# Masking the diagonal score blocks and swapping the maxima on other engines, in a hybrid decoder block

## The chip, the cores and the metric

The kernel runs on one core of a Trainium2 chip. The metric is the device time of one execution in microseconds (us). The core has a matrix engine (TensorE, PE in the rows; its weight loads are PEld) and three others: VectorE (DVE), ScalarE (ACT) and GpSimd (POOL). SyncE (SP) issues DMAs. Each engine works its own queue in order and waits for semaphores of the others. TensorE writes to PSUM, which VectorE and ScalarE read; GpSimd works in SBUF alone.

## The reference, cut to what matters

One decoder block on 1040 tokens (16 meta tokens and 1024 of the sequence) of width 1024: RMSNorm, one wide input projection, a pooling branch and an attention branch, gates, an output projection, and a final RMSNorm. The change is in the attention: 8 heads of width 64, with a forget gate that adds a difference of cumulated log gates to every score, and a causal mask:

```python
s = jnp.einsum('bqhd,bkhd->bhqk', qb, kb).astype(jnp.float32) * scale
s = s + c[:, :, q0:q1, None] - c[:, :, None, :q1]
valid = (k_idx <= q_idx) & ((k_idx >= pad) | (k_idx == q_idx))
s = jnp.where(valid, s, -jnp.inf)
p = jax.nn.softmax(s, axis=-1)
outs.append(jnp.einsum('bhqk,bkhd->bqhd', p.astype(vb.dtype), vb))
```

## The kernel before, in words

All products are made in pieces of reduced precision: a float32 operand is split into a high part (a copy on ScalarE) and a low part (a subtraction on VectorE or GpSimd), and three products (high with low, low with high, high with high) are summed in PSUM.

The attention is worked in 16 units: 4 pairs of heads, 2 heads in a pair, 2 halves of 512 queries (`Unit`, L537). Scores are kept transposed: 128 keys on the partitions, queries on the free axis. A unit of the first half has 5 blocks of keys, one of the second half 9. The queries of a half begin 16 tokens after a block of keys, so a block of keys on the diagonal covers 112 or 128 (for the last block 16) queries that need a mask; block `b` is computed from column `c0` on, and `d1` is where its masked columns end. In each unit:

- `qk(b)` (L557): two products into a bank `ps` of two (`psS`). Then the scores are moved to the tile `s` in SBUF with the key's gate sum `negc` added. The columns under the mask go through VectorE, which adds the constant tile `mask` in the same instruction (L579); the others go through ScalarE (L581). Then VectorE takes the running maximum over the blocks, `m` (L585, L586, L588). The last block of the second half (`own_keys`) is the 16 queries' own keys, with a mask of its own, `tail`.
- `maxes` (L590): the maximum over the 128 keys of each query. VectorE transposes `m` in squares of 32 (L593), reduces (L595), and joins the partitions: it copies the two halves of 64 partitions crosswise (L597), takes the maximum (L598), copies the quarters of 32 crosswise (L600), takes the maximum (L601), and broadcasts the result by a transpose into a PSUM bank, `pm` (L603).
- `soft(b)` (L606): VectorE subtracts `pm` (L612), ScalarE takes the exponential (L613) and the high part `ph` (L616), VectorE makes the low part `pl` (L617), and GpSimd adds into the unit's sums `acc` (L622 to L625). Two blocks later `av` (L629) multiplies both parts with the values into the bank `po`.
- `finish` (L636): ScalarE and VectorE join the halves of `po` (L640, L641) and it is stored; VectorE transposes and reduces the sums (L644, L646).

The scores of the next unit run between the softmax blocks of the current one (`merged`, L649). TensorE's order is as written. Between the attention's products it gets filler: projections (`g_proj`, L155) that `F.pull(ns)` (L355) draws from a queue for a given time, for instance `LM1` before and `LM2` behind the maxima. The projections use three banks `pj`, and each chunk of weights is split by ScalarE (L140) and GpSimd (L124, in four pieces). The order of instructions on the other engines, and of the DMAs on their queues, is made by a planner from data dependencies, the order of the text and its own costs of the instructions. The matmuls, their order and the calls of `F.pull` are the same in both kernels.

The mask constants are made at the start (L82 to L91).

Of the kernel before, what the change touches and what calls it, by code (L numbers as in the profile page):

```python
# [8 lines left out]
F32 = mybir.dt.float32  # L9
F32R = mybir.dt.float32r  # L10
AF = mybir.ActivationFunctionType
ALU = mybir.AluOpType
# [9 lines left out]
NEG = -1e30  # L22
KB = 128
# [29 lines left out]
def tile_hybrid_block(ctx, tc, x, meta, norm_g, w_in, b_forget, pool_w, pool_scale,  # L53
                      w_up_pool, w_up_attn, w_out, final_g, out):
    nc = tc.nc
# [8 lines left out]
    cst = ctx.enter_context(tc.tile_pool(name="cst", bufs=1))  # L64
# [14 lines left out]
    make_identity(nc, ident)  # L79
    epsp = cst.tile([128, 1], F32, name="epsp")  # L80
    nc.vector.memset(epsp, -0.5)
    mask = cst.tile([KB, KB], F32, name="mask")  # L82
    nc.vector.memset(mask, 0.0)
    nc.gpsimd.affine_select(out=mask, in_=mask, pattern=[[1, KB]], compare_op=ALU.is_ge, fill=NEG,
                            base=0, channel_multiplier=-1)
    tail = cst.tile([KB, OWN], F32, name="tail")
    nc.vector.memset(tail, 0.0)
    nc.gpsimd.affine_select(out=tail, in_=tail, pattern=[[1, OWN]], compare_op=ALU.is_ge, fill=NEG,
                            base=KB - OWN, channel_multiplier=-1)
    nc.gpsimd.affine_select(out=tail, in_=tail, pattern=[[0, OWN]], compare_op=ALU.is_ge, fill=NEG,  # L90
                            base=OWN - KB, channel_multiplier=1)  # L91
# [3 lines left out]
                            base=OWN - KB, channel_multiplier=1)  # L95
# [441 lines left out]
    class Unit:  # L537
# [19 lines left out]
        def qk(self, b):  # L557
            p, e, q0, t0, kb, c0 = self.p, self.e, self.q0, self.t0, self.kb[b], self.c0[b]
            h = 2 * p + e
            ka, qa, ql = KA[p, e], QA[p, e], QL[p, e]  # L560
            d1 = max(0, min(512, b * KB + KB - t0))
            own_keys = b == NB - 1
            if b == 0:
                self.m = ap_.tile([KB, 512], F32, name="m")
            m = self.m
            if b % 2 == 0:
                self.st = ap_.tile([KB, 2, 512], F32, name="S", tag="s", bufs=6)
            s = self.st[:, b % 2, :]
            self.S.append(s)
            ps = psS.tile([128, 512], F32, name="ps")  # L570
            k0 = KS[b]
            nc.tensor.matmul(ps[:kb, c0:], ka[:, k0:k0 + kb], qa[:, q0 + c0:q0 + 512], start=True, stop=False)  # L572
            nc.tensor.matmul(ps[:kb, c0:], ka[:, k0:k0 + kb], ql[:, q0 + c0:q0 + 512], start=False, stop=True)  # L573
            nb_ = negc[:kb, b, h:h + 1]
            f0 = max(d1, c0)
            if d1 > c0:
                j = t0 + c0 - b * KB
                mk = tail if own_keys else mask[:, j:j + d1 - c0]
                nc.vector.scalar_tensor_tensor(s[:kb, c0:d1], ps[:kb, c0:d1], nb_, mk, op0=ALU.add, op1=ALU.add)  # L579
            if f0 < 512:  # L580
                nc.scalar.activation(s[:kb, f0:], ps[:kb, f0:], AF.Identity, bias=nb_)  # L581
            S0 = self.S[0]
            if b == 1:
                if c0:
                    nc.vector.tensor_copy(m[:, :c0], S0[:, :c0])  # L585
                nc.vector.tensor_tensor(m[:, c0:], S0[:, c0:], s[:, c0:], op=ALU.max)  # L586
            elif b > 1:
                nc.vector.tensor_tensor(m[:kb, c0:], m[:kb, c0:], s[:kb, c0:], op=ALU.max)  # L588

        def maxes(self, extra=0.0):  # L590
            F.pull(LM1 + extra)
            mt = ap_.tile([KB, 512], F32, name="mt")
            nc.vector.transpose(mt, self.m)  # L593
            r, x, r2, y, mx = [sm.tile([128, 16], F32, name=n) for n in ("mr", "mx", "ms", "my", "mz")]
            nc.vector.tensor_reduce(r, mt.rearrange("p (j b) -> p j b", b=32), axis=AX.X, op=ALU.max)  # L595
            for a, b in ((0, 64), (64, 0)):
                nc.vector.tensor_copy(x[a:a + 64], r[b:b + 64])  # L597
            nc.vector.tensor_tensor(r2, r, x, op=ALU.max)  # L598
            for a, b in ((0, 32), (32, 0), (64, 96), (96, 64)):
                nc.vector.tensor_copy(y[a:a + 32], r2[b:b + 32])  # L600
            nc.vector.tensor_tensor(mx, r2, y, op=ALU.max)  # L601
            self.pm = psT.tile([128, 512], F32, name="pt")
            nc.vector.transpose(self.pm, mx[:, :, None].to_broadcast([128, 16, 32]))  # L603
            F.pull(LM2)
# [347 lines left out]
    for n, s in enumerate(steps):  # L952
# [12 lines left out]
        j, a = s  # L965
# [84 lines left out]
    for n in range(7):  # L1050
        if n < 6:
            prep(n + 1)
        ps = ba if n in (0, 2, 4, 6) else bb_
# [56 lines left out]
```

## Time and profile before

| | |
|---|---|
| median of 3 runs | 744.31 us (744.23 to 744.82) |
| the profiled execution's own time | 743.96 us |
| its span, first to last instruction | 742.2 us |
| TensorE busy | 731.2 us (99%) |
| VectorE busy | 533.2 us (72%) |
| ScalarE busy | 377.0 us (51%) |
| GpSimd busy | 332.8 us (45%) |
| granted TensorE clock, mean | 0.997 |

The span is the time between the first and the last instruction that the profiler saw on the core. Busy time is the time in which an engine has an instruction under way; matmuls are pipelined, so a TensorE that is busy need not be at its peak. The attention runs from about 84 to 505 us, with projections between its products. The time before belongs to the norm and the first projections, the time after it to the branches, gates and the output projection.

### The profile page before, as it was taken

How to read it: one execution, taken by the hardware profiler on the slowest of the kernel's cores; microseconds unless marked ns; L12 is line 12 of the kernel's file. 1: busy time of each engine (PE TensorE's matmuls, PEld its weight loads, DVE VectorE, ACT ScalarE, POOL GpSimd, SP SyncE). 2: the span in 40 equal slices, each digit the busy share in tenths (PEclk: the TensorE clock that was granted, in tenths of full speed). 3: DMA queues.
4: the chain of work that ended last, by engine and by line, in shares of the span. 5: the costliest groups of instructions: out<-in, count | busy, mean ns of one | idle time of the engine just before them, and what ended most of it. 6: DMA issues, size and time to landing. Idle time of an engine off the chain costs nothing.

```text
span 742.2 us, 10619 instructions
## 1 busy us (share of the span) xinstructions
PE 731.2 (99%) x3686; PEld 622.7 (84%) x3686; DVE 533.2 (72%) x991; ACT 377.0 (51%) x736; POOL 332.8 (45%) x390
## 2 busy tenths in 40 slices
PE   8999999999999999999999999999999999999996
PEld 5997999988888898889988888888887888888885
DVE  5653577668779877688797687686288554997975
ACT  6662556446557545556563564452545322526445
POOL 4331235456426446345355383183348043606743
PEclk9999999999999999999999999999999999999998
DMA  9301132231312212222323223229375357360006
GB/s 301 88 15 43 29 86 86 62 98 23 95 48 60 80 50 90 78 53 55 94 66 86 80 80 92 72 81 309 95 201 212 142 200 240 116 224 1 1 0 227
DMA packets 76424, 75.35 MB, mean 102 GB/s; under 512 B 9665, under 2 KB 60865, under 8 KB 76370
## 3 DMA queue, kind: packets, MB, share of 16 engines
q1 hardware_dynamic: 74496, 69.95, 30.8%
q10 hardware_dynamic: 1874, 4.72, 1.7%
q8 instruction: 29, 0.48, 0.3%
q14 instruction: 25, 0.20, 0.1%
HBM read 55.58 MB, written 19.07 MB: 101 GB/s over the span
## 4 chain that ended last, share of the span: by engine, by line
PE 87%; DVE 5%; ACT 1%; issue 1%; POOLq 0%; POOL 0%; ACTq 0%
PE pj L152 65%; PE pj L995 8%; PE po L633 5%; PE ps L573 2%; PE ps L572 2%; PE pt L995 2%; PE pj L486 1%; DVE S L612 1%; DVE pl L617 1%; DVE ka L266 0%; PE pj L279 0%; DVE pt L603 0%; ACT S L581 0%; DVE mt L593 0%; ACT whi L140 0%
## 5 line engine op out<-in xcount | busy, mean ns | idle before, releaser
L124 POOL TENSOR_TENSOR wlo<-raw,whi 128x256 fp32r<-128x256 f32 x148 | 121.7, 852 | 192.5 <-ACT whi L140 96.1
L152 PE MATMUL pj<-hh,whi 128*128 128x512 f32 (+4 forms) x768 | 178.4, 360 | 0.6 <-ACT hh L201 0.3
L152 PE MATMUL pj<-hl,whi 128*128 128x512 f32 (+4 forms) x768 | 177.1, 359 | 0.0
L152 PE MATMUL pj<-hh,wlo 128*128 128x512 f32 (+4 forms) x768 | 174.4, 358 | 0.0
L152 PEld LDWEIGHTS pj<-hh,wlo 128*128 128x128 f32 x768 | 132.3, 188 | 18.1
L152 PEld LDWEIGHTS pj<-hh,whi 128*128 128x128 f32 x768 | 131.5, 188 | 18.7 <-ACT hh L201 0.5
L152 PEld LDWEIGHTS pj<-hl,whi 128*128 128x128 f32 x768 | 131.6, 188 | 17.7
L617 DVE TENSOR_TENSOR pl<-S,ph 128x512 fp32r<-128x512 f32 (+4 forms) x112 | 87.1, 792 | 19.3 <-ACT ph L616 18.8
L625 POOL TENSOR_TENSOR acc<-acc,S 128x272 f32<-128x272 f32 (+4 forms) x80 | 76.7, 958 | 11.2 <-ACT S L613 6.0
L581 ACT ACTIVATE S<-ps,negc 128x400 f32<-128x400 f32 (+2 forms) x96 | 49.3, 515 | 44.0 <-DVE S L579 35.7
L613 ACT ACTIVATE S<-S 128x512 f32<-128x512 f32 (+4 forms) x112 | 49.5, 478 | 33.7 <-DVE S L612 33.5
L616 ACT ACTIVATE ph<-S 128x512 fp32r<-128x512 f32 (+4 forms) x112 | 52.2, 480 | 15.8 <-PE po L633 14.4
L588 DVE TENSOR_TENSOR m<-m,S 128x272 f32<-128x272 f32 (+4 forms) x80 | 41.3, 517 | 23.8 <-ACT S L581 22.0
L140 ACT ACTIVATE whi<-raw 128x1024 fp32r<-128x1024 f32 x37 | 39.1, 1056 | 32.2 <-PE pj L152 27.8
L612 DVE TENSOR_TENSOR S<-S,pt 128x512 f32<-128x512 f32 (+4 forms) x112 | 51.9, 498 | 0.8
L836 DVE TENSOR_TENSOR rl<-pj,rl 128x512 f32<-128x512 f32 x32 | 22.0, 689 | 28.0 <-PE pj L152 28.0
L579 DVE SCALAR_TENSOR_TENSOR S<-ps,negc,mask 128x128 f32<-128x128 f32 (+2 forms) x72 | 23.7, 330 | 22.5 <-PE ps L573 22.3
L317 ACT ACTIVATE st<-pj 128x512 f32<-128x512 f32 x40 | 23.7, 593 | 28.1 <-PE pj L152 18.6
L633 PE MATMUL po<-pl,V 128*128 128x512 f32 (+4 forms) x112 | 37.6, 336 | 0.1
L573 PE MATMUL ps<-ql,ka 128*128 128x512 f32 (+4 forms) x112 | 37.5, 334 | 0.0
L572 PE MATMUL ps<-qa,ka 128*128 128x512 f32 (+4 forms) x112 | 36.0, 322 | 0.6 <-ACT S L581 0.5
L995 PE MATMUL pj<-opy 128*128 128x512 f32 (+1 forms) x168 | 36.3, 375 | 0.0
(187 smaller groups left out, 1134.2 us busy)
## 6 DMA issues: line engine op xcount, KB each, us to landing
raw<-in_w_in_dram SPq DMA_DIRECT2D x40, 512.0 KB, 3.9
sp_gp<-st SPq DMA_DIRECT2D x16, 256.0 KB, 2.0
sp_ga<-st SPq DMA_DIRECT2D x16, 256.0 KB, 2.0
rl<-sp_gp SPq DMA_DIRECT2D x8, 512.0 KB, 5.2
rl<-sp_ga SPq DMA_DIRECT2D x8, 512.0 KB, 4.5
W<-in_w_out_dram SPq DMA_DIRECT2D x8, 512.0 KB, 4.8
xr<-in_x_dram SPq DMA_DIRECT2D x8, 512.0 KB, 4.1
xt<-in_x_dram SPq DMA_DIRECT2D x7, 512.0 KB, 8.1
```

What stands on the lines that cost most here:

```text
L124: ins = nc.gpsimd.tensor_tensor(out[:, c:c + 256], x[:, c:c + 256], y[:, c:c + 256], op=op)
L152: nc.tensor.matmul(ps, a, b, start=(i == 0), stop=(i == len(seq) - 1))
L572: nc.tensor.matmul(ps[:kb, c0:], ka[:, k0:k0 + kb], qa[:, q0 + c0:q0 + 512], start=True, stop=False)
L573: nc.tensor.matmul(ps[:kb, c0:], ka[:, k0:k0 + kb], ql[:, q0 + c0:q0 + 512], start=False, stop=True)
L581: nc.scalar.activation(s[:kb, f0:], ps[:kb, f0:], AF.Identity, bias=nb_)
L612: nc.vector.tensor_tensor(s[:kb, c0:], s[:kb, c0:], self.pm[:kb, c0:], op=ALU.subtract)
L613: exps.append(nc.scalar.activation(s[:kb, c0:], s[:kb, c0:], AF.Exp))
L616: nc.scalar.activation(ph[:kb, c0:], s[:kb, c0:], AF.Copy)
L617: dves.append(nc.vector.tensor_tensor(pl[:kb, c0:], s[:kb, c0:], r32(ph[:kb, c0:]), op=ALU.subtract))
L625: nc.gpsimd.tensor_tensor(acc[:kb, c0:], acc[:kb, c0:], s[:kb, c0:], op=ALU.add)
L633: nc.tensor.matmul(self.po[:, c0:], v, r[:kb, c0:], start=(b == 0 and i == 0), stop=(b == self.nb - 1 and i == 1))
L995: nc.tensor.matmul(ps, pick(A_, k, p)[:, i * 128:(i + 1) * 128], pick(B_, k, q)[:, c0:c1], start=start and n == 0, stop=n == 11, skip_grou ...
```

## The change

The masked columns of a block are no longer moved by VectorE with the mask added. ScalarE moves the whole block, from `c0` to the end, and GpSimd then overwrites, in place in SBUF, the columns `c0` to `d1` where the key is later than the query with -1e30 (an affine select: it keeps an element where an affine form of partition and column is not negative). The `own_keys` block stays on VectorE. The constant `mask` goes. In `maxes` the six crosswise copies of a unit become activations of ScalarE. The rest is the same.

```diff
-    mask = cst.tile([KB, KB], F32, name="mask")
-    nc.vector.memset(mask, 0.0)
-    nc.gpsimd.affine_select(out=mask, in_=mask, pattern=[[1, KB]], compare_op=ALU.is_ge, fill=NEG,
-                            base=0, channel_multiplier=-1)
...
             nb_ = negc[:kb, b, h:h + 1]
-            f0 = max(d1, c0)
-            if d1 > c0:
-                j = t0 + c0 - b * KB
-                mk = tail if own_keys else mask[:, j:j + d1 - c0]
-                nc.vector.scalar_tensor_tensor(s[:kb, c0:d1], ps[:kb, c0:d1], nb_, mk, op0=ALU.add, op1=ALU.add)
-            if f0 < 512:
-                nc.scalar.activation(s[:kb, f0:], ps[:kb, f0:], AF.Identity, bias=nb_)
+            if own_keys:
+                nc.vector.scalar_tensor_tensor(s[:, c0:], ps[:, c0:], nb_, tail, op0=ALU.add, op1=ALU.add)
+            else:
+                nc.scalar.activation(s[:, c0:], ps[:, c0:], AF.Identity, bias=nb_)
+                if d1 > c0:
+                    nc.gpsimd.affine_select(out=s[:, c0:d1], in_=s[:, c0:d1], pattern=[[1, d1 - c0]],
+                                            compare_op=ALU.is_ge, fill=NEG, base=t0 + c0 - b * KB,
+                                            channel_multiplier=-1)
...
             for a, b in ((0, 64), (64, 0)):
-                nc.vector.tensor_copy(x[a:a + 64], r[b:b + 64])
+                nc.scalar.activation(x[a:a + 64], r[b:b + 64], AF.Copy)
             nc.vector.tensor_tensor(r2, r, x, op=ALU.max)
             for a, b in ((0, 32), (32, 0), (64, 96), (96, 64)):
-                nc.vector.tensor_copy(y[a:a + 32], r2[b:b + 32])
+                nc.scalar.activation(y[a:a + 32], r2[b:b + 32], AF.Copy)
```

## Rows read from the trace of the kernel before

**Rows 1.** The page, busy us by engine: share of the span, instructions.
```profile
PE 731.2 (99%) x3686; PEld 622.7 (84%) x3686; DVE 533.2 (72%) x991; ACT 377.0 (51%) x736; POOL 332.8 (45%) x390
```
**Rows 2.** Windows: start:end, length, busy us (instructions) by engine, TensorE's clock, DMA.
```profile
84.00:505.00 421.00, 420.09 (x2151) 366.30 (x2151) 328.46 (x686) 230.33 (x478) 202.87 (x229) 1.00 0.26 74
```
**Rows 3.** Waits of TensorE, 84 to 505 us: total us, times, longest.
```profile
PE ps L572 <- ACT S L581: 0.5, 1, 0.5
PE pj L152 <- DVE V L285: 0.2, 1, 0.2
```
**Rows 4.** Tile ps: idle before its instructions, by releaser (us, times).
```profile
  DVE S L579: 35.7, 35
...
  ACT S L581: 1.9, 4
```
**Rows 5.** The page, groups: count, busy us, mean ns, idle before by releaser.
```profile
L579 DVE SCALAR_TENSOR_TENSOR S<-ps,negc,mask 128x128 f32<-128x128 f32 (+2 forms) x72 | 23.7, 330 | 22.5 <-PE ps L573 22.3
```
**Rows 6.** Groups by form, 84 to 490 us, VectorE's crosswise copies.
```profile
L600 DVE COPY my<-ms 32x16 f32<-32x16 f32 x64 | 11.2, 175 | 1.1
...
L597 DVE COPY mx<-mr 64x16 f32<-64x16 f32 x32 | 8.2, 255 | 0.8
```
**Rows 7.** Groups by form, 84 to 490 us, ScalarE.
```profile
L581 ACT ACTIVATE S<-ps,negc 128x512 f32<-128x512 f32 x32 | 21.8, 685 | 8.1 <-PE ps L573 7.8
...
L581 ACT ACTIVATE S<-ps,negc 128x16 f32<-128x16 f32 x16 | 4.3, 269 | 8.2 <-DVE S L579 8.2
...
L613 ACT ACTIVATE S<-S 128x16 f32<-128x16 f32 x16 | 3.3, 208 | 3.2 <-DVE S L612 3.2
```
**Rows 8.** Timeline of GpSimd, 0 to 12 us: start, length, instruction, idle before.
```profile
1.32 0.29 POOL L84 TENSOR_SCALAR_AFFINE_SELECT mask<-mask 128x128 f32<-128x128 f32 x1
1.56 0.20 POOL L88 TENSOR_SCALAR_AFFINE_SELECT tail<-tail 128x16 f32<-128x16 f32 x1
...
5.96 0.55 POOL L114 TENSOR_TENSOR rstd<-rstd,epsp 128x1 f32<-128x1 f32 x1 [4.08 <-DVE rstd L113]
```
**Rows 9.** Timeline of GpSimd, 370 to 402 us.
```profile
384.22 6.16 POOL L625 TENSOR_TENSOR acc<-acc,S 128x512 f32<-128x512 f32 x4
```
**Rows 10.** Lines L617 and L612: count, ns shortest/median/longest, first and last start.
```profile
L617 DVE TENSOR_TENSOR pl<-S,ph x112: 166/732/1787, 99.5 to 498.0; 128x512 fp32r<-128x512 f32 x48, 128x400 fp32r<-128x400 f32 x16, 128x272 fp32r<-128x272 f32 x16, 128x144 fp32r<-128x144 f32 x16
...
L612 DVE TENSOR_TENSOR S<-S,pt x112: 156/564/691, 95.8 to 489.2; 128x512 f32<-128x512 f32 x48, 128x400 f32<-128x400 f32 x16, 128x272 f32<-128x272 f32 x16, 128x144 f32<-128x144 f32 x16
```
**Rows 11.** Timeline of VectorE, 370 to 402 us.
```profile
373.72 0.71 DVE L593 STREAM_TRANSPOSE mt<-m 128x512 f32<-128x512 f32 x1
...
375.99 0.71 DVE L644 STREAM_TRANSPOSE mt<-acc 128x512 f32<-128x512 f32 x1
...
376.73 0.69 DVE L646 TENSOR_REDUCE sr<-mt 128x16 f32<-128x512 f32 x1
...
378.40 0.73 DVE L603 STREAM_TRANSPOSE pt<-mz 128x512 f32<-128x512 f32 x1
...
382.28 0.69 DVE L617 TENSOR_TENSOR pl<-S,ph 128x512 fp32r<-128x512 f32 x1
```
**Rows 12.** Timeline of VectorE, 214 to 234 us.
```profile
217.47 0.71 DVE L593 STREAM_TRANSPOSE mt<-m 128x512 f32<-128x512 f32 x1
...
224.68 0.73 DVE L603 STREAM_TRANSPOSE pt<-mz 128x512 f32<-128x512 f32 x1
...
230.66 1.69 DVE L617 TENSOR_TENSOR pl<-S,ph 128x512 fp32r<-128x512 f32 x1
```
**Rows 13.** Timeline of TensorE, 229 to 234 us.
```profile
231.96 0.39 PE L633 MATMUL po<-ph,V 128*128 128x512 f32 x1
232.41 0.50 PE L633 MATMUL po<-pl,V 128*128 128x512 f32 x1
```
**Rows 14.** Timeline of ScalarE, 370 to 402 us.
```profile
376.31 0.59 ACT L640 ACTIVATE t<-po 64x512 f32<-64x512 f32 x1 [1.26 <-PE po L633]
```
**Rows 15.** Timeline of TensorE, 384 to 387 us.
```profile
385.59 0.39 PE L633 MATMUL po<-pl,V 128*128 128x512 f32 x1
```

## The prediction, made before the changed kernel ran

> **What bounds the kernel now.** The page's list of engines comes first: TensorE is busy 731.2 of 742.2 us of the span [rows 1]. A busy TensorE need not be at its peak, so I looked at the stretch the change touches, the attention from 84 to 505 us, in the view by windows: TensorE is busy 420.09 of 421.00 us at a granted clock of 1.00, the 2.4 GHz level, with VectorE at 328.46, ScalarE at 230.33 and GpSimd at 202.87 [rows 2]. The reader is to see two things there. TensorE has 0.91 us of idle time in all, and every other engine has at least 92 us. The list of TensorE's waits in that stretch has two entries, 0.5 us on a score eviction of ScalarE and 0.2 us on a value eviction of VectorE [rows 3]; counted with the weight loads, the waits on score evictions are 1.9 us in four places [rows 4]. TensorE's own program is written by hand and the change edits no matmul and no amount of filler, so its sequence stays. The change can therefore act in two ways only: take away some of the 0.9 to 2 us, or make new waits of TensorE. What is worth asking is how much slack each wait of TensorE has, not how much work each engine has.
>
> **The change part by part.**
>
> *Removed from VectorE.* 72 masked evictions, 23.7 us [rows 5], and per unit two copies of 255 ns and four of 175 ns, 32 and 64 in all, 8.2 + 11.2 = 19.4 us [rows 6]. Together 43.1 us of VectorE's 328.5 in the stretch. All of it lies beside TensorE's work; of itself it is worth nothing. What it takes away is a wait of ScalarE: 35.7 us in 35 places, in which ScalarE waited for VectorE's part of the same score bank before it did its own [rows 4].
>
> *Added on ScalarE.* The 16 evictions each of 400, 272, 144 and 16 columns become ones of 512, 400, 272 and 144; by the rows that telescopes to 16 x (685 - 269) ns = 6.7 us. Eight new ones of 16 columns cost 8 x 269 ns = 2.2 us [rows 7]. The 96 copies are not in the trace on this engine. The nearest row is an activation of 16 columns from SBUF to SBUF, 208 ns; the copy as VectorE had it, 175 ns, and the 269 ns of the eviction bound it. I take 208: 20.0 us, with 17 to 26 as ends. In all +29 us, to 259 of 421. No bank of projections waits for this long: a bank is one of three, and ScalarE still has 160 us free.
>
> *Added on GpSimd.* 48 selects of 128 x 128, 16 of 112 and 8 of 16 columns. The trace has the operation at the start, 0.29 us for 128 columns and 0.20 for 16 [rows 8]: 64 x 0.29 + 8 x 0.20 = 20.2 us if undisturbed. It ran there with VectorE nearly idle, so that is the lower end. In the attention a GpSimd instruction with two inputs takes 1.54 us for 512 columns (four in 6.16 us [rows 9]), so a quarter of that, 0.39 us, is the upper end for 128 columns: 27 us. Both fit into 421 - 203 = 218 us.
>
> *Sharing between VectorE and GpSimd.* VectorE's subtraction with both inputs in SBUF takes 166 to 1787 ns; the one whose second input is in PSUM stays at 156 to 691 ns over the same shapes [rows 10]. So more GpSimd work stretches VectorE's two-input instructions, by at most what is added, 20 to 27 us, against 43 us taken away.
> The Trainium skill, "SBUF — State Buffer", section "Who interferes with whom", says that such a VectorE instruction and a GpSimd instruction that reads SBUF exclude each other for a whole instruction, whichever began second. Rows 10 agree; it speaks against the change, and by it VectorE's net relief would be 16 to 23 us instead of 43, with TensorE's time the same.
>
> *The masked block's path.* Before: TensorE, VectorE 0.34 us, then ScalarE's rest of the block (0.27 to 0.59), then the maximum on VectorE, because ScalarE waited for VectorE. After: TensorE, ScalarE (0.38 to 0.69), GpSimd 0.29, the maximum. The lengths agree within 0.1 us where GpSimd is free. The score bank is released after ScalarE alone, 0.2 us sooner. I take 0, between -0.2 and, where GpSimd has just begun a sum, +1.5 [rows 9]. Behind the waiting maximum on VectorE stand the subtractions of the current unit, for which ScalarE and then TensorE's value products wait.
>
> *The swaps at a unit's end.* Before, from the transpose of the maxima at 373.72 to the end of the broadcast at 378.40 + 0.73, 5.4 us pass; in between VectorE also transposes and reduces the sums, 0.71 + 0.69 us, which are not of the chain [rows 11]. VectorE's copies are 2 x 0.255 + 4 x 0.175 = 1.2 us of it. After: 6 x 0.21 = 1.26 us on ScalarE and four handovers between engines. One handover, from VectorE's end at 230.66 + 1.69 to TensorE's start at 232.41, is 0.06 us [rows 12, 13]; so +0.3 us if nothing overlaps. If the two other instructions fall into the gaps that VectorE now has, the chain is 1.1 us shorter. If ScalarE is held in order by its eviction of the values, which sat 1.26 us for TensorE and took 0.59 [rows 14], it is up to 2.1 us longer. I take +0.3, the plain sum.
> Who waits for it: the first value products of the unit. In the unit after 373.72, the low half of its first block is ready at 382.28 + 0.69 = 382.97 [rows 11] and TensorE takes it at 385.59 [rows 15], 2.6 us later; of the eight units with nine blocks seven are like that (2.3 to 4.8 us). The exception is the unit of 217.47: there the chain took until 224.68 + 0.73, 7.9 us, with query evictions between [rows 12], and TensorE waits: the value product at 231.96 is followed only at 232.41 by the one that needs the low half, instead of some 0.23 us later [rows 13]. So +0.3 us costs 0.3 us in one unit and nothing in the others.
>
> *Waits that might go.* The four on score evictions, by their tile, are of the first full-width blocks of a nine-block unit, while ScalarE does exponentials; these blocks have no mask. I credit 0.1 us, at most the 0.91 of the idle time.
>
> *The start.* The mask's constant and its select (0.29 us) go; GpSimd then sat 4.08 us idle anyway [rows 8]. Nothing.
>
> **Sum.** 743.96 us is the profiled execution's own time (span 742.2 and 1.8 around it): +0.3 - 0.1 = 744.2. The runs shown have their median at 744.31, 0.35 above that execution, so I predict 744.5 us.
>
> **Rivals.**
> *The maxima wait for GpSimd (slower).* GpSimd works its queue in order, and it runs four sums one after the other, 6.16 us [rows 9]. If a select is queued behind more of them than the one in progress, VectorE's maximum waits, and behind it the subtractions. For: those four run from 384.22 to 390.4, while the scores of the next unit are made; against: GpSimd is idle for half of the stretch [rows 2], and VectorE has 43 us less to do. The tight unit at 217.47 pays every microsecond; the others only beyond 2.3 to 4.8. A delay of 2 us gives 746.5, one of two sums, 3.1 us, gives 3.1 + 7 x 0.5 = 6.6, thus 751. It decides from 1.5 us in the tight unit. The swaps on ScalarE held up by 2.1 us end at the same price.
> *VectorE's relief is worth something (faster).* If the whole idle time of TensorE in the stretch goes, 0.91 us, with a shorter chain in the tight unit, the time is 744.31 - 0.9 = 743.4; with the 1.9 us of all waits on score evictions, weight loads included, 742.4. For: ScalarE no longer waits 35.7 us for VectorE. Against: TensorE's waits are at blocks that have no mask, and ScalarE gets 29 us more.
> *The planner reorders elsewhere.* The order on all engines but TensorE comes from a planner whose costs change with the instructions. A weight split or a gate load planned later would show as a wait of a projection; nothing in the trace sizes it; TensorE's slack at the projections (0.2 us of waits on 421 [rows 3]) speaks against more than 1 us: up to 745.5.
>
> **How the numbers follow.** About 0.2% (1.5 us) is what a measurement of this kernel can tell from no change. Forecast 0.62, GpSimd or the swaps in the way 0.20, relief 0.10, reordering 0.08. Faster by over 0.2% (under 742.8) needs nearly all of the waits to go: 0.07. Slower by over 0.2% (over 745.8): nearly all of the first rival and a little of the third, 0.21. The range 743.2 to 747.0 leaves the deep ends of both.
>
> **What would show it.** Right: VectorE's busy time down by 20 to 43 us, ScalarE's up by 29, GpSimd's by 20 to 27, and TensorE's idle time in the attention within 1 us of 0.91. Wrong: new entries among TensorE's waits for the low halves or the score banks; a long wait of the maximum on the select; a chain from the maxima's transpose to their broadcast over 7 us in several units; or a select far from 0.3 us.

## The result and the profile after

The changed kernel takes 746.79 us (median of 7 runs, 745.89 to 747.61) against 744.31 (7 runs, 743.83 to 744.85): ratio 1.0033, 95% interval 1.0023 to 1.0043, 1.7 to 3.2 us slower. Two later comparisons gave 1.0033 [1.0021, 1.0046] and 1.0037 [1.0025, 1.0050]. Medians in this document are of executions in the fast state alone: one of the six with the selects alone (800.7 us, granted clock 0.852) and one of the twelve with block 0 masked as before (893.9 us, 0.754) are not counted. The time lies in the forecast range. The likeliest case, no change, is not what happened: it came out as the rival named slower, in another place than the one named.

The page of the profiled execution (span 745.1 us, own time 746.79) answers to rows 1:

```profile
PE 732.5 (98%) x3686; PEld 624.1 (84%) x3686; DVE 478.4 (64%) x822; ACT 406.9 (55%) x840; POOL 344.8 (46%) x461
```

The view by windows for the attention, as rows 2 (window, length, then busy time of PE, PEld, DVE, ACT, POOL, granted clock, DMA share, GB/s):

```profile
84.00:505.00 421.00, 418.33 (x2142) 364.84 (x2141) 272.08 (x518) 259.11 (x581) 215.71 (x301) 1.00 0.25 72
```

VectorE lost 56.4 us, ScalarE got 28.8 more, GpSimd 12.8. TensorE's idle time, 421 less its busy time, went from 0.91 [rows 2] to 2.67 us. That is 1.8 of the 2.5 us. TensorE's waits show where (engine, tile and line, what it waited for, us in all, times, longest):

```profile
PE ps L568 <- ACT S L574: 1.1, 2, 0.7
PE pj L148 <- DVE V L281: 0.6, 1, 0.6
PE po L630 <- ACT ph L613: 0.6, 1, 0.6
PE po L630 <- DVE pl L614: 0.4, 1, 0.4
```

Against rows 3 the last two are new, and they stand 0.8 us apart, in one unit:

```profile
331.44 0.39 PE L568 MATMUL ps<-qa,ka 128*128 128x512 f32 x1
...
349.31 0.39 PE L630 MATMUL po<-ph,V 128*128 128x272 f32 x1 [0.56 <-ACT ph L613]
350.10 0.39 PE L630 MATMUL po<-pl,V 128*128 128x272 f32 x1 [0.40 <-DVE pl L614]
```

This is a unit of nine blocks whose softmax runs while the scores of the next unit, one of five blocks, are made. A measure that does not depend on when the execution began: from the scores of block 0 of the next unit to the value product with the low half of the 272-column block, 350.10 - 331.44 = 18.66 us pass. In the kernel before it was 347.13 - 330.07 = 17.06:

```profile
330.07 0.39 PE L572 MATMUL ps<-qa,ka 128*128 128x512 f32 x1
...
347.13 0.29 PE L633 MATMUL po<-pl,V 128*128 128x272 f32 x1
```

So 1.6 us are lost there. Set against each other one by one, the matmuls of the two profiled executions show the rest: 0.8 us by 17 us, before the attention (the kernel before, run again, moved by 0.5 there by itself), -0.4 at a masked score block of the first unit (88 us), 0.9 at the score banks of the second unit (100 to 104 us), 0.35 at a value eviction (175 us), and -0.3 at the unit that the prediction named as tight (232 us). With -0.1 after it this is the whole difference of 2.85 us between the two spans.

What happens ahead of the loss is in the timelines (start, length, instruction, and in brackets the idle time just before it and what ended it). GpSimd:

```profile
335.37 2.66 POOL L622 TENSOR_TENSOR acc<-acc,S 128x512 f32<-128x512 f32 x2
337.98 0.27 POOL L576 TENSOR_SCALAR_AFFINE_SELECT S<-S 128x112 f32<-128x112 f32 x1
```

ScalarE:

```profile
334.73 0.69 ACT L574 ACTIVATE S<-ps,negc 128x512 f32<-128x512 f32 x1
...
341.24 0.48 ACT L259 ACTIVATE ka<-pj 64x384 fp32r<-64x384 f32 x1 [3.13 <-DVE ka L262]
```

VectorE:

```profile
338.29 1.33 DVE L582 COPY m<-S 128x112 f32<-128x112 f32 x1 [2.85 <-POOL S L576]
339.63 0.30 DVE L609 TENSOR_TENSOR S<-S,pt 128x144 f32<-128x144 f32 x1
339.86 0.69 DVE L614 TENSOR_TENSOR pl<-S,ph 128x512 fp32r<-128x512 f32 x1
...
345.80 0.57 DVE L583 TENSOR_TENSOR m<-S 128x400 f32<-128x400 f32 x1 [1.77 <-POOL S L576]
```

ScalarE has block 0 out of PSUM at 335.42. The select stands behind two sums until 337.98. VectorE's next instruction is the copy of that block into the maxima, so VectorE stands idle for 2.85 us, with a subtraction and a low half behind the copy; a key eviction of VectorE further back (L262) then holds ScalarE for 3.13 us. At the maximum of block 1, whose select stands behind four more sums, VectorE waits again, 1.77 us. The unit had little slack: in the kernel before the low half of its 272-column block was written 0.31 us ahead of the product that takes it (345.85 + 0.97 = 346.82, against 347.13):

```profile
345.85 0.97 DVE L617 TENSOR_TENSOR pl<-S,ph 128x272 fp32r<-128x272 f32 x1
```

Over the whole attention VectorE's waits read:

```profile
DVE m L585 <- POOL S L576: 51.6, 41, 4.1
DVE m L582 <- POOL S L576: 20.8, 7, 4.6
...
DVE m L583 <- POOL S L576: 15.7, 8, 4.3
```

88 us at 56 of the 72 selects. Most of it is harmless: TensorE waits for a half of the softmax in one unit alone. There a softmax stands behind the maximum, and TensorE is close behind that softmax.

### The profile page after: what moved, and what is told of

It is laid out like the page before. It is cut to its first block, busy times and chain, and to the rows that moved or that the text cites. A ratio compares the mean times of both kernels' runs of the same rounds, so it can differ in the third digit from the quotient of the medians.

```text
span 745.1 us, 10828 instructions
## 1 busy us (share of the span) xinstructions
PE 732.5 (98%) x3686; PEld 624.1 (84%) x3686; DVE 478.4 (64%) x822; ACT 406.9 (55%) x840; POOL 344.8 (46%) x461
## 4 chain that ended last, share of the span: by engine, by line
PE 83%; issue 4%; DVE 3%; ACT 2%; POOL 2%; POOLq 0%; ACTq 0%; DVEq 0%
PE pj L148 63%; PE pj L992 8%; PE po L630 5%; PE pt L992 2%; PE ps L569 2%; PE ps L568 2%; PE pj L482 1%; POOL wlo L120 1%; DVE S L609 1%; DVE pl L614 0%; DVE ka L262 0%; ACT S L610 0%; PE pj L275 0%; POOL acc L622 0%; DVE pt L600 0%
## 5 line engine op out<-in xcount | busy, mean ns | idle before, releaser
L120 POOL TENSOR_TENSOR wlo<-raw,whi 128x256 fp32r<-128x256 f32 x148 | 118.0, 826 | 120.5 <-ACT whi L136 101.0
L614 DVE TENSOR_TENSOR pl<-S,ph 128x512 fp32r<-128x512 f32 (+4 forms) x112 | 74.6, 680 | 19.8 <-ACT ph L613 19.4
L574 ACT ACTIVATE S<-ps,negc 128x512 f32<-128x512 f32 (+4 forms) x104 | 57.8, 560 | 43.4 <-PE ps L569 40.4
L622 POOL TENSOR_TENSOR acc<-acc,S 128x272 f32<-128x272 f32 (+4 forms) x80 | 72.9, 912 | 11.6 <-ACT S L610 6.9
L585 DVE TENSOR_TENSOR m<-m,S 128x272 f32<-128x272 f32 (+4 forms) x80 | 38.8, 485 | 59.9 <-POOL S L576 51.6
L576 POOL TENSOR_SCALAR_AFFINE_SELECT S<-S 128x128 f32<-128x128 f32 (+2 forms) x72 | 21.2, 297 | 76.3 <-ACT S L574 72.9
L630 PE MATMUL po<-ph,V 128*128 128x512 f32 (+4 forms) x112 | 36.3, 324 | 0.6 <-ACT ph L613 0.6
```

Source lines behind the costliest of these rows:

```text
L120: ins = nc.gpsimd.tensor_tensor(out[:, c:c + 256], x[:, c:c + 256], y[:, c:c + 256], op=op)
L574: nc.scalar.activation(s[:, c0:], ps[:, c0:], AF.Identity, bias=nb_)
L614: dves.append(nc.vector.tensor_tensor(pl[:kb, c0:], s[:kb, c0:], r32(ph[:kb, c0:]), op=ALU.subtract))
L622: nc.gpsimd.tensor_tensor(acc[:kb, c0:], acc[:kb, c0:], s[:kb, c0:], op=ALU.add)
L630: nc.tensor.matmul(self.po[:, c0:], v, r[:kb, c0:], start=(b == 0 and i == 0), stop=(b == self.nb - 1 and i == 1))
```

## Experiments

TensorE's idle time is 421 us less its busy time between 84 and 505 us; the next column is the stretch of 17.06 us measured above. The changed kernel, run twice more, gave 2.68 and 2.71 us of idle time, and 18.69 us both times.

| kernel | idle | scores to low half | ratio to before [95%] |
|---|---|---|---|
| before | 0.91 | 17.06 | 1 |
| changed | 2.67 | 18.66 | 1.0033 [1.0023, 1.0043] |
| selects alone | 4.95 | 20.40 | 1.0065 [1.0044, 1.0086] |
| swaps alone | 1.01 | 17.06 | 0.9994 [0.9982, 1.0005] |
| block 0 masked as before | 1.67 | 17.06 | 1.0006 [0.9994, 1.0018] |
| selects ahead in GpSimd's queue | 5.42 | 18.40 | 1.0071 [1.0057, 1.0085] |
| every select twice | 4.64 | 19.43 | 1.0077 [1.0064, 1.0090] |
| mask added by VectorE in SBUF | 0.86 | 17.06 | 0.9994 [0.9985, 1.0003] |
| the same for block 0 alone | 1.14 | 17.86 | 1.0011 [1.0002, 1.0020] |
| seven copies later in VectorE's queue | 1.65 | 17.06 | 1.0009 [0.9999, 1.0018] |

**The two halves of the change.** The selects alone, from the changed kernel (both lines of copies):

```diff
-                nc.scalar.activation(x[a:a + 64], r[b:b + 64], AF.Copy)
+                nc.vector.tensor_copy(x[a:a + 64], r[b:b + 64])
...
```

> The masked evictions go to ScalarE and the selects to GpSimd as in the changed kernel; the six crosswise copies of a unit stay on VectorE. Theory G (the maxima on VectorE wait for selects that stand behind sums and weight splits in GpSimd's in-order queue): this half carries the loss; 746.5 to 748 us, a wait of line 582 to 585 on the select of over 2 us near 340 us and TensorE waits of 1 us or more on ph or pl there. Theory S (the copies on ScalarE, held in its order, carry the loss): within 0.5 us of the kernel before, 744.0 to 744.8. Theory L (29 us more work on ScalarE, in proportion to what each part adds): 9 of 29 us of it are here, so a third of the loss, about 745.1.

The swaps alone are the same edit the other way round in the kernel before.

> The masks stay as in the kernel before; only the six crosswise copies of a unit go to ScalarE. Theory G: no loss, and the chain from the transpose of the maxima to their broadcast falls from 5.0 to about 4.1 us in most units, so the one unit that waited for a low half at 232 us no longer does: 743.8 to 744.4 us. Theory S: 746 to 747. Theory L: two thirds of the loss, about 746.0.

749.84 against 744.67 us, and 744.55 against 744.67. The loss is in the selects, and larger than theory G's 746.5 to 748; the swaps alone cost nothing. With the selects they gain: 749.8 becomes 746.8 (two chips, befores of 744.7 and 744.3). They shorten the chain. From the start of the transpose to the start of the broadcast the 16 units take 3.74 us in the mean, against 4.69 before and 4.67 with the selects alone; in the unit of the loss 3.40 against 4.74 and 4.74, so its softmax begins earlier. That this is what they gain was not tried apart: with the selects alone VectorE is also busier in the attention (294.4 us against 272.1), and in the profiled execution some 1.6 us of the loss are a lower clock (last section). In the unit that answers to rows 11, VectorE's timeline after the change reads:

```profile
375.48 0.71 DVE L590 STREAM_TRANSPOSE mt<-m 128x512 f32<-128x512 f32 x1
...
377.10 0.70 DVE L641 STREAM_TRANSPOSE mt<-acc 128x512 f32<-128x512 f32 x1
...
378.67 0.67 DVE L643 TENSOR_REDUCE sr<-mt 128x16 f32<-128x512 f32 x1
...
379.91 0.73 DVE L600 STREAM_TRANSPOSE pt<-mz 128x512 f32<-128x512 f32 x1
```

4.4 us from transpose to broadcast, start to start, against 4.7 [rows 11]: the transpose and the reduction of the sums have moved into the gaps in which ScalarE copies. In the unit of rows 12 it is 218.64 to 223.77, 5.1 us against 7.2.

**The kernel before once more**, to see what a start is worth.

> The kernel before once more, for a second trace of it: in the changed kernel's trace TensorE is 0.8 us later by 17 us already, in the norm's first transposes, where the change only leaves out a constant. If that is the landing time of the first loads, this trace differs from the first one there by some tenths of a us too; if it comes from the change, TensorE's first transposes stand at 10.34 and 16.02 us again within 0.1.

745.0 us, span 743.3: 0.5 us later by 17 us of the execution, with the same kernel. So most of the 0.8 us can come without the change.

**Block 0 of the five-block units masked as before**, all other selects kept:

```diff
...
+            elif self.half == 0 and b == 0:
...
+                nc.vector.scalar_tensor_tensor(s[:, c0:d1], ps[:, c0:d1], nb_, mask[:, j:j + d1 - c0], op0=ALU.add, op1=ALU.add)
...
+                    nc.scalar.activation(s[:, d1:], ps[:, d1:], AF.Identity, bias=nb_)
...
```

> The changed kernel, but block 0 of the eight units with 5 blocks is masked as before, on VectorE out of PSUM; 64 of the 72 selects and all copies stay as changed. Theory G, in its narrow form: the 1.5 to 1.8 us that TensorE loses between 339 and 350 us come from the select of this block, for which VectorE sat 2.85 us, so they go: 744.7 to 745.5 us. If instead any select may be caught, the loss moves to another unit and the time stays at 746 to 747.5. Theories S and L: no change, 746.5 to 747.

745.33 us against 744.67, and the two waits on the halves are gone from TensorE's list:

```profile
PE ps L572 <- ACT S L583: 1.1, 2, 0.7
PE pj L152 <- DVE V L285: 0.6, 1, 0.6
```

One of these eight selects carries the loss of that unit. Against the old path of its block three things are new: ScalarE moves the whole block, and later; GpSimd stands between; and the copy into the maxima, in VectorE's queue, waits for GpSimd. The next runs take these apart.

**Selects ahead of the sums on GpSimd.** Sums and weight pieces traced behind a select stay behind it in GpSimd's queue:

```diff
...
+            ins = ahead(nc.gpsimd.tensor_tensor(out[:, c:c + 256], x[:, c:c + 256], y[:, c:c + 256], op=op))
...
+                ahead(nc.gpsimd.tensor_tensor(acc[:kb, c0:], acc[:kb, c0:], s[:kb, c0:], op=ALU.add))
...
```

> The changed kernel, with one thing more: every sum and every piece of a weight split that the text has behind a select also stands behind it in GpSimd's queue. No work is added. Theory G in the form that the place in the queue costs (a ready select stands behind sums): VectorE's longest waits on selects between 335 and 348 us go, TensorE's loss of 1.5 us there goes, 744.8 to 745.6 us. Rival P (the path through two engines costs, whatever the queue: ScalarE moves the whole block late, behind query evictions, and VectorE waits for that): the waits stay, now on ScalarE's eviction, 746 to 747.5. Rival W (weight splits held back for selects make TensorE wait for a projection's low weights): new TensorE waits on GpSimd, over 747.

**Every select twice** (the second finds nothing to change):

```diff
+                    for _ in range(2):
+                        nc.gpsimd.affine_select(out=s[:, c0:d1], in_=s[:, c0:d1], pattern=[[1, d1 - c0]],
...
```

> The changed kernel with each select made twice (the second finds nothing more to do): 21 us more work on GpSimd, and 0.3 us more on the path of every masked block. Theory G by place in the queue: the select's own length is small beside the waits; the loss over the changed kernel is 0.3 to 1 us, 747 to 748. Rival D (the operation's own time on the path of 72 blocks costs): the loss of the change about doubles, 749 or more. If GpSimd's load as such cost (21 us already in the change), it also about doubles.

**The changed kernel again**, on the same chip:

> The changed kernel once more, on the chip of these runs, as the one to compare the two others with. 746 to 747.6 us, and the same waits of TensorE near 340 to 350 us: 0.6 us for ph and 0.4 us for pl of the same unit, within 0.1.

Putting the selects first takes the copy's wait from 20.8 us to 4.1, yet the time rises to 749.65, where theory G gave 744.8 to 745.6:

```profile
DVE m L589 <- POOL S L583: 4.1, 7, 1.2
```

TensorE then waits elsewhere:

```profile
PE ps L575 <- ACT S L581: 3.1, 3, 1.5
PE pj L155 <- DVE V L288: 1.3, 1, 1.3
PE po L637 <- DVE pl L621: 0.9, 1, 0.9
```

No wait of TensorE is on GpSimd, which speaks against rival W. This order changes GpSimd's queue in all units, and VectorE is busier, 297.5 us against 272.1. So it doesn't acquit the queue; it shows that holding back the sums and weight pieces costs more than it gives. Every select twice gives 750.2 us, against 746.75 for the changed kernel beside it: the second pass of the 72 selects costs 3.5 us, more than the change with its first pass did (746.75 - 744.42 = 2.3). Theory G's 747 to 748 was missed; the time is that of rival D, or of GpSimd's load (749 or more). The run can't part them from G: in the unit of the loss a low half now stands ahead of the copy in VectorE's queue, VectorE waits 2.15 us at block 1's maximum, and the clock fell (last section).

**GpSimd taken out of the path, ScalarE's eviction kept.** VectorE adds the mask in place in SBUF, for all blocks:

```diff
-                    nc.gpsimd.affine_select(out=s[:, c0:d1], in_=s[:, c0:d1], pattern=[[1, d1 - c0]],
...
+                        nc.vector.tensor_tensor(s[:, c0:d1], s[:, c0:d1], mask[:, j:j + d1 - c0], op=ALU.add)
...
```

> The changed kernel, but the mask is put on in place by VectorE (it adds the constant tile to the block's columns in SBUF), for all 72 blocks: ScalarE still moves whole blocks and makes the copies, GpSimd is out of the path. Theory G (GpSimd's queue on the path costs): 744.4 to 745.4 us, and no wait of TensorE for ph or pl. Rival P (the whole block moved late by ScalarE costs, whoever masks): 746 to 747.5, with the wait of the maximum now put down to ScalarE's eviction.

and for block 0 of the five-block units alone:

> The same for block 0 of the eight units with 5 blocks alone; the other 64 selects stay on GpSimd. Theory G: as with block 0 back on its old path (745.35), 744.9 to 745.7 us. Rival P: 746 to 747.5, since block 0 still waits for ScalarE to move it whole. If GpSimd's order of work in general costs, and not this block: between the two, with new losses elsewhere.

All blocks: 743.96 against 744.29 us, which can't be told from no change; the ratio is that of the swaps alone. TensorE's waits are as short as before:

```profile
PE pj L152 <- DVE V L285: 0.4, 1, 0.4
PE ps L572 <- ACT S L578: 0.4, 1, 0.4
```

ScalarE's eviction of the whole block is not the cause, then. VectorE's timeline in the place of the loss says more (scores of block 0 at 329.88):

```profile
335.09 0.30 DVE L617 TENSOR_TENSOR S<-S,pt 128x144 f32<-128x144 f32 x1
335.31 1.54 DVE L622 TENSOR_TENSOR pl<-S,ph 128x512 fp32r<-128x512 f32 x1
336.77 1.31 DVE L590 COPY m<-S 128x112 f32<-128x112 f32 x1
```

The copy starts 6.89 us after the scores, no earlier than in the changed kernel (338.29 - 331.44 = 6.85), and yet nothing is lost. The maximum itself is not what comes too late. What differs is that VectorE works ahead of it.

Block 0 alone gives 745.40 us against 744.29, in theory G's range, but half of the loss in that stretch stays (17.86 us), with one of TensorE's waits:

```profile
PE po L638 <- DVE pl L622: 0.4, 1, 0.4
```

The mask takes VectorE 1.32 us there, and the maximum of block 1, whose select stands behind four sums, still waits:

```profile
343.71 0.58 DVE L591 TENSOR_TENSOR m<-S 128x400 f32<-128x400 f32 x1 [1.78 <-POOL S L584]
```

It starts 13.56 us after the scores; that was 14.36 in the changed kernel and 12.10 with block 0 on its old path. By the timelines the delay is handed on: what holds VectorE up also holds up the exponentials, the sums behind them, and the next select behind the sums.

**The same copies, later in VectorE's queue.** Seven of the eight copies are put behind the low half that was written just before them in the program. GpSimd keeps its selects, and no instruction of another engine changes its place:

```diff
-    exps, dves = [], []
+    exps, dves = [], []; late = lambda ins: after(ins, dves[-1]) if dves else None
...
-                    nc.vector.tensor_copy(m[:, :c0], S0[:, :c0])
+                    late(nc.vector.tensor_copy(m[:, :c0], S0[:, :c0]))
```

> The changed kernel, with the seven copies of block 0's maxima (five-block units) put behind the low half that was written just before them; nothing else on any engine is in another order. If the loss is what stands behind the waiting copy in VectorE's queue, VectorE's wait of the copy on the select falls from 20.8 us to under 8, the time from block 0's scores to the low half of the 272-column block (18.66 us, 17.06 before) falls to 17.1 to 17.9, TensorE's idle time in 84 to 505 us from 2.67 to 1.1 to 1.9, and the ratio to 1.000 to 1.002. If the loss is the longer path of the maximum over GpSimd, or GpSimd's load beside VectorE, nothing of that moves: 18.6, 2.6 and 1.003, or more since the maximum comes later.

Beside it the changed kernel:

> The changed kernel as it is, timed beside the run with the later copies, to compare the two on one chip: ratio 1.002 to 1.0045 as twice before, TensorE's idle time 2.6 to 2.7 us.

745.01 us, beside 746.95 for the changed kernel and 744.04 before. VectorE, in the place of the loss (scores of block 0 at 331.70):

```profile
335.73 0.30 DVE L609 TENSOR_TENSOR S<-S,pt 128x144 f32<-128x144 f32 x1
336.24 1.24 DVE L614 TENSOR_TENSOR pl<-S,ph 128x512 fp32r<-128x512 f32 x1 [0.20 <-ACT ph L613]
...
339.36 1.31 DVE L582 COPY m<-S 128x112 f32<-128x112 f32 x1 [0.17 <-POOL S L576]
```

GpSimd, there:

```profile
335.65 3.00 POOL L622 TENSOR_TENSOR acc<-acc,S 128x512 f32<-128x512 f32 x2
338.60 0.73 POOL L576 TENSOR_SCALAR_AFFINE_SELECT S<-S 128x112 f32<-128x112 f32 x1
```

The select is no earlier (6.9 us after the scores, 6.5 in the changed kernel) and still stands behind two sums, and the copy starts later, at 7.7 us. The wait has shrunk to 0.17 us, the 17.06 us are back, and 1.9 of 2.9 us are won. VectorE's other waits on selects stayed (51.2 and 19.2 us, against 51.6 and 15.7), so by themselves they cost nothing in that stretch. That settles the larger part: the loss is the work behind a waiting instruction at the head of VectorE's queue. 0.74 us stay in TensorE's idle time above before's 0.91, at the score banks of the second unit and at one value eviction; which of the changed instructions sets those was not tried. With the mask added in SBUF by VectorE, TensorE's waits at score banks are 0.4 us for all blocks and none for block 0 alone, against 1.1 here.

## Where the prediction was right and where it went wrong, step by step

- **What bounds the kernel** held: a version's time follows TensorE's idle time (the two grow together within 1 us, but for selects alone and every select twice, where the clock fell as well, below), not any engine's load. VectorE was freed of 56 us and the kernel got slower.
- **The sizes.** ScalarE +29 us forecast, +28.8 measured. Its copies took 213 and 214 ns against 208 taken, in ScalarE's groups by line:

```profile
L597 ACT ACTIVATE my<-ms 32x16 f32<-32x16 f32 x64 | 13.7, 213 | 7.0 <-DVE ms L595 6.4
...
L594 ACT ACTIVATE mx<-mr 64x16 f32<-64x16 f32 x32 | 6.9, 214 | 21.5 <-DVE mr L592 21.2
```

- The selects took 21.2 us, mean 297 ns, within 20 to 27. GpSimd's busy time rose by 12.8 us only, since its weight pieces took 93.8 us instead of 96.9 and 80 of its sums 72.9 instead of 76.7. In 41 of 72 cases an eviction ended GpSimd's idle time ahead of the select, so the engine was waiting for it; 28 of the other 31 have no idle time before them, and stood behind other work of GpSimd. Rows from the page's group, then from the list of what ended the idle time before the line's instructions:

```profile
L576 POOL TENSOR_SCALAR_AFFINE_SELECT S<-S 128x128 f32<-128x128 f32 (+2 forms) x72 | 21.2, 297 | 76.3 <-ACT S L574 72.9
```

```profile
  ACT S L574: 72.9, 41
```

- **Sharing between VectorE and GpSimd** came out with the other sign. VectorE's relief was forecast as 20 to 43 us and was 56.4: the low halves, slowed by GpSimd before, went from a mean of 792 ns to 680, 87.1 to 74.6 us over the same 112, before and after:

```profile
L617 DVE TENSOR_TENSOR pl<-S,ph 128x512 fp32r<-128x512 f32 (+4 forms) x112 | 87.1, 792 | 19.3 <-ACT ph L616 18.8
```

```profile
L614 DVE TENSOR_TENSOR pl<-S,ph 128x512 fp32r<-128x512 f32 (+4 forms) x112 | 74.6, 680 | 19.8 <-ACT ph L613 19.4
```

By the rule of the Trainium skill, "SBUF — State Buffer", section "Who interferes with whom", the prediction had 16 to 23 us of relief. The single instructions still look as it says: low halves take 166 to 1786 ns after, and the select 193 to 677. The sum by it was wrong because it takes the overlap in time as given. In the attention, the time in which GpSimd works and VectorE is idle went from 41.8 to 88.7 us; but with the selects alone it is 77.3 and the low halves still take 760 ns, so this is not shown to be the whole reason.
- **The swaps**: +0.3 us was taken, with -1.1 as the good end. Where nothing overlaps (the first unit) the chain went from 4.2 to 4.5 us, the plain sum. Elsewhere the good end is nearer (in the mean of the 16 units -0.95 us, start to start), because the two instructions on the sums do fall into the gaps; and in the tight unit of rows 12 and 13 the wait is gone: the low half is ready at 227.73 + 0.69 = 228.42 and taken at 231.63.
- **Waits that might go** were credited with 0.1 us. One of the four was read wrongly: it stands at 88.42 us, at a masked block of the first unit, and there 0.4 us were won. The second unit's score banks lost 0.9.
- **The masked block's path, taken as 0, is the step that failed.** Its lengths "agree within 0.1 us where GpSimd is free", and the end given for a busy GpSimd was one sum, +1.5. In the place of the loss two sums stood ahead, 2.56 us. More than the size, the price was wrong: the step went on to say that subtractions stand behind the waiting maximum, and did not price them. In that unit they cost 1.6 us. Two of the prediction's signs of being wrong came with it: a new wait of TensorE for a low half, and a long wait of the maximum on the select.
- **The rival that came true** had the mechanism right ("VectorE's maximum waits, and behind it the subtractions") but not its place. That its price for 2 us, 746.5, is near the measured time is luck: it charges the tight unit, which gained 0.3 us, while 1.6 of the measured 2.5 us are in another unit and the rest is elsewhere. Its price for 3.1 us, 751, is too high by the same trace: of the seven other units only three have less slack than that (2.27, 2.52 and 2.62 us), which gives 1.9 us in place of 7 x 0.5. Slack was read at each unit's first block alone, where the maxima's chain ends. The waiting maximum comes in the middle of a unit's softmax and shows at its last blocks, and there one unit had 0.31 us. In hindsight 0.20 was too little for it: 28 selects straight behind other work, sums of 1.3 to 1.5 us among it, and one place without slack, were enough.
- **VectorE's relief is worth something** fell: the mask in SBUF by VectorE leaves 0.86 us of idle time, against 0.91. **Reordering by the planner** could not be seen apart; the changed places in VectorE's queue are part of the mechanism, since the copy stood ahead of work that was ready.

## What to carry to other kernels

Handing a short operation to an engine with half its time free cost little in work here and more in order: the instruction that needs its result sits in an in-order queue, and what it holds up there has to be priced. So look at which ready instructions stand behind the new wait, and take slack from the last consumer that those feed, in every unit, not from the first one. If a result may come late, put its consumer later in its engine's queue; here that won 1.9 of 2.9 us with no other engine's order changed.

## What the runs showed of the hardware

In two kernels that stall TensorE more, its granted clock fell to its lower level, 1.2 GHz, behind the stalls. In the profiled execution with the selects alone TensorE was busy 2.94 of 4 us, then 1.28 of 2 us, and then the clock was 0.56 and 0.50 (windows, columns as above):

```profile
346.00:350.00 4.00, 2.94 (x15) 2.19 (x14) 1.87 (x4) 0.89 (x3) 1.77 (x5) 1.00 0.00 0
350.00:352.00 2.00, 1.28 (x6) 0.89 (x6) 1.31 (x3) 1.77 (x4) 1.04 (x3) 1.00 0.00 0
352.00:354.00 2.00, 1.67 (x4) 1.38 (x5) 1.48 (x4) 1.18 (x5) 2.00 (x3) 0.56 0.00 0
354.00:355.60 1.60, 1.60 (x5) 1.30 (x4) 1.36 (x5) 0.19 (x2) 0.71 (x3) 0.50 0.15 17
355.60:358.00 2.40, 2.40 (x13) 1.93 (x12) 2.29 (x7) 0.60 (x1) 0.00 (x0) 0.99 0.74 207
```

Eight or so matmuls of 512 columns followed each other at about 0.43 us instead of 0.23, some 1.6 us in all, on top of the idle time. With every select twice the clock is 0.50 between 352 and 354 us, and the mean clock 0.995 in four of five executions (750.20 to 750.55 us); in the fifth it is 0.999 (749.31 us). The changed kernel's profiled execution has 0.998. The changed kernel, busy 3.15 of 4 and 1.90 of 2 us in the same windows, kept 1.00.
